# Attention stage of a one-core encoder layer: two heads in one PSUM bank, three masks moved to the selection stage, two more dense blocks woven in, and a choice among 17 orders

## The chip, the core and the metric

The kernel runs on one NeuronCore of one Trainium2 chip. A core has a matrix engine (TensorE, in the profile PE, with its weight loads as PEld), three engines for elementwise work (VectorE or DVE, ScalarE or ACT, GpSimd or POOL), and a SyncE (SP) that here issues every DMA. Each engine runs its own instructions in the order in which they were written and waits on semaphores for the others. The metric is the device time of one execution in microseconds (us); lower is better.

## The reference, cut to what matters

One layer of a streaming encoder: a SwiGLU feed-forward, a mixer with two attention branches, a second feed-forward. All in float32, 1024 tokens, width 1024. The change lies in the mixer:

```python
def fox_attention(q, k, v, log_f):            # 8 heads of 64, causal, with a forget bias
    F = jnp.cumsum(log_f, axis=1)
    ...
        s = jnp.einsum('bqhd,bkhd->bhqk', qb, k) * scale
        s = s + Fq[..., None] - F[:, :, None, :]
        s = jnp.where(mask, s, -jnp.inf)
        p = jax.nn.softmax(s, axis=-1)
        return jnp.einsum('bhqk,bkhd->bqhd', p, v)

def dsa_attention(q, k, v, iq, ik, iw, top_k):  # 8 heads, one shared k and v; each query attends
    ...                                         # to the 256 keys with the best index score
        score = jnp.einsum('bqh,bqhk->bqk', iwb, jax.nn.relu(dots))
        score = jnp.where(admissible[None], score, -jnp.inf)
        _, sel = lax.top_k(score, top_k)
    ...

merged = sigmoid(ga) * (ya @ w_br_fox) + sigmoid(gb) * (yb @ w_br_dsa)
return merged @ w_out
```

## The kernel before

**Two layers of program.** The functions of the kernel are generators that say what is computed, step by step. `weave` (line 2036) advances several of them side by side, in given proportions. While the plan is on, no instruction is emitted: `Plan.take` (215) records each as a `Task` with the tiles that it reads and writes and a rank, which is its number plus `nc.behind` (a lag that `behind`, 2072, sets for work of less urgency). At the end of a stage `Plan.flush` (519) orders all its tasks: `place` (318) simulates the engines with the durations of `takes` (450) or `length` (298), takes at each step the task that can start first, and breaks ties by rank. A task that needs a new tile may be placed only if its rank is at most `window` (600 here) above the lowest unplaced rank. `flush` makes two orders (with `takes` and no hold, with `length` and a hold of 0.05), passes each through `replay` (474), and emits the one whose TensorE ends first. All calls of one kind go through line 557, so the profile shows this line everywhere and rows are told apart by tile.

**Precision.** Each float32 operand is split into a rounded part hi (written by ScalarE) and a rest lo (VectorE, or GpSimd for some weights). A product is three matmuls: hi by hi, hi by lo, lo by hi (`mm3`, 589).

**The stages around the change.** Before the attention stage lies the *selection stage* (2433 to 2447): TensorE multiplies dense projections, while `topk` (977) finds the 256th best index score of each query. Query blocks 2 to 4 are searched bit by bit on VectorE (`rounds`), blocks 5 to 7 in two halves of 16 bits on ScalarE (`both`); the thresholds go into tile `thr`. Blocks 0 and 1 need no search, since they have at most 256 keys.

The *attention stage* (2453 to 2486) weaves three generators over 300 steps:
- attention: FoX's four pairs of heads, then DSA's four. For each pair and each two query blocks (j from 0 to 3) `att_scores` (1289) makes scores in PSUM tiles `p`, adds the forget bias or the mask with a minimum on VectorE (tile `pr`, `mn`), takes exp on ScalarE and normalizes on GpSimd. `att_values` (1337), for one head at a time, transposes `pr` through PSUM tiles `pt`, splits them into `pth` and `ptl` (`pzh` and `pzl` on the diagonal), and multiplies with the values into a PSUM tile `py` of which it uses 256 of 512 columns. The result leaves through tile `yt` (64x256) to `d_y` in HBM.
- `masks` (1076), in 40 parts of the 300 and 600 ranks behind: from the thresholds the masks of blocks 2 to 7, on VectorE, with tiles `tke`, `tky`, `tkg`, `tkn`. DSA needs them.
- dense work, 200 ranks behind, in 144 parts: `gates` (1214), 16 blocks of 24 matmuls of 512 columns for the second half of the tokens, then `Branches.first` (1943). The latter loads FoX's results from `d_y`, splits them into 16 tiles `h`, which are those that held the gates' operands, and multiplies the first two of eight output blocks of the FoX branch, gated with `d_gate`. Its raw data (weights `wbr`, results, gates) pass through two buffers `wr`; a weight's split goes over ScalarE (`wh`) and GpSimd (`wl`).

`pt`, `py` and the dense products share four PSUM banks (tag `pj`); `p` has the other four.

The *next stage* begins with `Branches.rest` (1969): blocks 2 to 7 of the FoX branch, the DSA results, the eight blocks of the DSA branch, then `w_out`. Its tensors use the memory that the attention stage leaves.

Of the kernel before, what the change touches and what calls it, by code (L numbers as in the profile page):

```python
# [22 lines left out]
D = 1024  # L23
# [171 lines left out]
class Plan:  # L195
# [19 lines left out]
    def take(self, engine, op, a, kw):  # L215
        if not self.on:
            return getattr(getattr(self.tc.nc, engine), op)(*map(real, a), **{n: real(v) for n, v in kw.items()})
        t = Task(len(self.tasks), engine, op, a, kw)
        t.rank, t.group = t.i + self.behind, max(0, self.group) if engine == "tensor" else 0
        self.tasks.append(t)  # L220
        writes = [v for v in (a[0], kw.get("accum_out")) if isinstance(v, View)]
        reads = [v for v in list(a[1:]) + [w for n, w in kw.items() if n != "accum_out"] if isinstance(v, View)]
        before = set()
        for views, write in ((reads, False), (writes, True)):
            for v in views:
                r = v.region()
# [24 lines left out]
        shape = list(out.shape)  # L251
        t.n = int(np.prod(shape[1:]))
        if op == "tensor_reduce":
            t.n = int(np.prod(a[1].shape[1:]))
        t.bytes = 4 * int(np.prod(shape))
        t.port = engine in ("vector", "gpsimd") and "accum_out" not in kw and not any(
            v.tile.pool.space == PSUM for v in reads + writes)
        if engine == "tensor":
            m = a[2] if op == "matmul" else a[1]
            t.exact = m.tile.dt in (F32R, BF16) or any(o[0] == "bitcast" and F32R in o[1] for o in m.ops)  # L260
            t.paired = op == "matmul" and a[1].region()[:1] == ((64, 128),)
            t.half = op == "matmul" and a[1].region()[:1] in (((64, 128),), ((0, 64),))
# [253 lines left out]
            free[e] = s + d  # L516
        return free

    def flush(self, keep=()):

        for x in keep:
            x.tile.uses += 1
# [16 lines left out]
            self.free, self.port, self.wire, self.kept = dict(st[3]), dict(st[4]), st[5], dict(st[6])  # L539

        at, best = state(), None
        for c in range(2):
            back(at)
            self.exact = not c
            order = self.place(0.05 * c)
            if order is None:
                continue
            free = self.replay(order, at[3], at[5])
            cost = free["tensor"]
            if best is None or cost < best[0]:  # L550
                best = (cost, order, state(), free)
# [188 lines left out]
def part8(w, c):  # L740

    return tuple(t[:, c * 128:c * 128 + 128] for t in w)
# [234 lines left out]
def topk(k, tmp):  # L977
# [90 lines left out]
    for i, _ in enumerate(rounds()):  # L1068
        if i % 2 == 0:
            next(b, None)  # L1070
        yield
    for _ in b:
        yield


def masks(k, tmp):


    nc = k.nc
    for qb in range(2, 8):  # L1080
        w = (qb + 1) * 128
        t, s = k.thr[:, qb - 2:qb - 1], k.s[qb]
        e, y = (tmp.tile([128, T], BF16, tag="tk" + x, name="tk" + x, bufs=1)[:, :w] for x in "ey")
        g = tmp.tile([128, T], F32, tag="tkg", name="tkg", bufs=1)[:, :w]
        need = tmp.tile([128, 2], F32, tag="tkn", name="tkn", bufs=2)
        nc.vector.tensor_scalar(e, s, t, None, op0=ALU.is_gt, op1=ALU.add, accum_out=need[:, 0:1])
        nc.vector.tensor_scalar(need[:, 1:2], need[:, 0:1], -1.0, float(TOPK), op0=ALU.mult, op1=ALU.add)
# [201 lines left out]
def att_scores(k, p, two, j, ps2):  # L1289
# [39 lines left out]
    for h in range(2):  # L1329
# [1 line left out]
            w, c = (2 * j + i + 1) * 128, 4 + 2 * i + h  # L1331
            nc.gpsimd.tensor_scalar(t[:, :w], t[:, :w], mn[:, c:c + 1], 1.0, op0=ALU.mult, op1=ALU.mult)
        yield
    two.pr = pr


def att_values(k, p, hd, j, pr, ps_t, ps_y):
    nc = k.nc
    py = ps_y()

    def pv(g, hi, lo):
        for i in range(2):
            kb = 2 * g + (1 - i if g == j else i)
            c = slice(i * 256, i * 256 + 256)
            end = g == j and i == 1
            if not end:
                nc.tensor.matmul(py[:, :256], hd.v(kb, 128), hi[:, c], start=g == 0 and i == 0, stop=False)
            nc.tensor.matmul(py[0:64, :256], hd.v(kb, 64), lo[:, c], start=False, stop=False)
            if end:
                nc.tensor.matmul(py[:, :256], hd.v(kb, 128), hi[:, c], start=False, stop=True)  # L1350

    last = None
    for g in range(j + 1):

        pt = ps_t(F32)
        if g == j:
            hi, lo = k.pz[k.pz_i % len(k.pz)]
# [11 lines left out]
        if last:  # L1369
            pv(*last)  # L1370
        yield
        last = (g, hi, lo)
    pv(*last)
    t = p.tile([64, 256], F32, tag="yt", name="yt", bufs=2)
    nc.scalar.activation(t, py[64:128, :256], AF.Copy)
    nc.vector.tensor_add(t, py[0:64, :256], t)
    nc.sync.dma_start(hd.y[:, j * 256:j * 256 + 256], t)
    yield


# [14 lines left out]
def pair_heads(k, p, kind, pr, ps_t, out):  # L1395
# [14 lines left out]
    else:  # L1410
# [2 lines left out]
        k.q2 = yield from two_heads(k, k.ap0, "qs", 4, lambda i: t[:, i, :], 2, None, ps_t)  # L1413
        two.kk = k.dks
        two.addend = lambda h, qb: k.mask[qb]
    two.q, two.heads = k.q2, []
    for h in range(2):
        hd = Head()
        hd.y = out[pr][h * 64:h * 64 + 64, :]
        if kind == "fox":  # L1420
            hd.v = lambda b, n, v=v[h]: v[:, b, 0:n]
        else:
            hd.v = lambda b, n: k.dvs[:, b, 0:n]
        two.heads.append(hd)
# [4 lines left out]
def attention(k, p, kind, npairs, out, ps2, ps_t, ps_y):  # L1429
# [3 lines left out]
    for pr in range(npairs):  # L1433
        two = k.ready
        prep = pair_heads(k, p, kind, pr + 1, ps_t, out) if pr + 1 < npairs else iter(())
        for j in range(4):
            yield from att_scores(k, p, two, j, ps2)
            for u in pend:
                yield from att_values(k, p, *u, ps_t, ps_y)
            pend = [(two.heads[h], j, two.pr[h]) for h in range(2)]  # L1440
            if j > 1:
                for _ in range(4):
                    next(prep, None)
# [109 lines left out]

PAIRS = NF // 2
NG = 6


class Operands:
# [369 lines left out]
class Branches:  # L1928
# [14 lines left out]
    def first(self, ws, ring, ptile):  # L1943

        k, nc = self.k, self.k.nc
        self.w, self.t = [next(ws) for _ in range(2)], []
        yield
        for pr in range(4):
            t = ring.raw()
            nc.sync.dma_start(t, k.d_y[0][pr])  # L1950
            for hf in range(2):
# [1 line left out]
                split(k, a, b, t[:, hf * H:hf * H + H])  # L1953
                self.y[hf].append((a, b))
                yield
        for i in range(2):
            g = ring.raw()
            nc.sync.dma_start(g, k.d_gate[i])
            for hf in range(2):
                ps = ptile()  # L1960
                self.product(ps, lambda c: part8(self.w[i], c), 0, hf)
                self.gated(g[:, hf * H:hf * H + H], ps)
                yield
            self.t.append(g)

    def kept(self):
        return [t for y in self.y for p in y for t in p] + [t for w in self.w for t in w] + self.t
# [1 line left out]
    def rest(self, pt1):  # L1969
# [14 lines left out]
            w = k.wq.split(k.wq.raw(self.wbr[d], br, home))  # L1984
            return lambda c: tuple(x[:, c % 4 * 128:c % 4 * 128 + 128] for x in w)

        for d in range(2, 8):
            w = half(d, 0, "c")
            for hf in range(2):
                t[d, hf] = gated(0, d, hf, w)  # L1990
            if d == 2:
# [107 lines left out]
def layer(tc, xT, c, pos, ada_w, ada_b, ng, inv, w13a, w2a, w_a, w_f, w_q, w_g, fb, fg, dg, wbr, wout, w13b, w2b, out):  # L2099
    with ExitStack() as es:  # L2100
# [51 lines left out]
        k.d_qkv = [dram([128, 8, 384], f"d_qkv{i}") for i in range(4)]  # L2152
        k.d_dq = [dram([128, 8, 128], f"d_dq{i}") for i in range(4)]
        k.d_gate = dram([16, 128, T], "d_gate")
        k.d_y = [[dram([128, T], f"d_y{b}{i}") for i in range(4)] for b in range(2)]

        s1 = ExitStack()
# [275 lines left out]
        with ExitStack() as ph:  # L2433
# [14 lines left out]
        ws.parts, ws.n = [(d_wg[b], D, r2) for b in range(2, 16)] + [(wbr[b], D, r2) for b in range(2)], 1  # L2448
        fox.close()
        s1.close()  # L2450

# [4 lines left out]
        with ExitStack() as ph:  # L2456
            ap = pool(ph, "att", True)
            ap.lay(("zero", 128, F32, 1), ("pzh", H, F32R, 2), ("pzl", H, F32R, 2), ("pth", H, F32R, 3), ("ptl", H, F32R, 3),
                   ("yt", 256, F32, 2), ("f", T, F32, 2), ("vst", T, F32R, 2), ("qs", T, F32R, 2), ("mn", 8, F32, 6))
            mp = pool(ph, "masks", True)  # L2460
            ap.p.tile([128, 16], F32, name="pad4")
            pt = lambda dt: pq.tile([128, H], dt, tag="pj", name="pt", bufs=4)
# [19 lines left out]
                yield from attention(k, ap, "dsa", 4, k.d_y[1], p2, pt, py)  # L2482

            br = Branches(k, wbr)
            weave((chain(attention(k, ap, "fox", 4, k.d_y[0], p2, pt, py), dsa()), 300), (behind(nc, masks(k, mp), 600), 40), (behind(nc, chain(gates(k, ws, 1, GateTiles(ap, py)), br.first(ws, r2, py)), 200), 144))
            nc.flush(br.kept())
        ps.close()
        s3.close()

# [136 lines left out]
```

## Time and profile before

| | us |
|---|---|
| median of 3 runs | 2172.49 |
| lowest, highest | 2171.11, 2172.92 |
| the profiled execution | 2171.82 |
| its span, from the first to the last instruction | 2170.1 |

The profile covers one execution. A row of the grouped views names engine, operation, output<-inputs and shape; times on the axis count from the span's start. TensorE is counted as busy from a matmul's start to its modelled end, so neighbouring matmuls overlap and a busy share near 100% doesn't say that matmuls follow each other as closely as they can. The number of matmuls in a stretch says that. The selection stage ends at about 1006 us, the attention stage with `Branches.first` at about 1362 us. The last gate of the attention stage, the first load into `wr` after it and what follows there are read from the views by tile; the rows stand where they are used.

### The profile page before, as it was taken

To read this page: it belongs to the slowest core of one execution; us is meant where nothing else is said; L and a number is where in the kernel's file an instruction comes from. 1 tells how busy PE (TensorE), PEld (TensorE's weight loads), DVE (VectorE), ACT (ScalarE), POOL (GpSimd) and SP (SyncE) were. 2 spreads that over 40 slices of the span, in tenths; PEclk is the share of its full clock that TensorE was granted. 3 is DMA by queue.
4 is the path that set the end of the run, shared out by engine and by line. 5 is a ranking of instruction groups with operands and counts; after the bars stand their busy time and mean duration, and the time that the engine had idled before them with its cause. 6 is when DMAs were issued, how large, how long until landed. Compare 5 with 4: busy or idle time off the path is not lost. (4 is left out here: it accounts for less than half of the span.)

```text
span 2170.1 us, 31523 instructions
## 1 busy us (share of the span) xinstructions
PE 2130.4 (98%) x10700; PEld 1777.6 (82%) x10700; DVE 1616.0 (74%) x3095; ACT 1130.3 (52%) x2103; POOL 221.3 (10%) x229
## 2 busy tenths in 40 slices
PE   7999999999999999999999999999999999999999
PEld 5887888887888989997778877888788888888887
DVE  7977887789876499964996777598866756558665
ACT  5744444445455466785766777244543333334443
POOL 0000212210010110111342333000000000000000
PEclk9999999999999999999999999999999999999999
DMA  9245887799521444356343312696123532367521
GB/s 337 99 136 180 274 286 260 243 366 337 158 81 60 146 153 141 103 188 221 108 151 106 125 48 82 233 358 189 58 81 126 174 122 83 107 232 273 175 73 39
DMA packets 208622, 364.15 MB, mean 168 GB/s; under 512 B 29622, under 2 KB 57270, under 8 KB 208460
## 3 DMA queue, kind: packets, MB, share of 16 engines
q1 hardware_dynamic: 208460, 362.13, 49.2%
q8 instruction: 84, 1.38, 0.3%
q14 instruction: 78, 0.64, 0.1%
HBM read 265.85 MB, written 96.20 MB: 167 GB/s over the span
## 5 line engine op out<-in xcount | busy, mean ns | idle before, releaser
L557 PE MATMUL bs<-h,wh 128*128 128x512 f32 x1728 | 533.6, 391 | 2.2 <-ACT bs L557 1.3
L557 ACT ACTIVATE wh<-wr 128x512 fp32r<-128x512 f32 (+1 forms) x330 | 207.5, 639 | 347.6 <-PE bs L557 158.4
L557 PEld LDWEIGHTS bs<-h,wh 128*128 128x128 f32 x1728 | 323.6, 188 | 73.1 <-ACT bs L557 4.3
L557 PE MATMUL b<-h,wh 128*128 128x512 f32 x1088 | 339.0, 392 | 3.2 <-ACT z L557 1.6
L557 PE MATMUL bs<-h,wl 128*128 128x512 f32 x864 | 335.5, 390 | 0.6 <-DVE wl L557 0.6
L557 DVE TENSOR_TENSOR wl<-wr,wh 128x512 fp32r<-128x512 f32 x308 | 210.6, 701 | 121.4 <-ACT wh L557 116.7
L557 PEld LDWEIGHTS b<-h,wh 128*128 128x128 f32 x1088 | 204.4, 188 | 48.0 <-ACT z L557 2.4
L557 PE MATMUL b<-h,wl 128*128 128x512 f32 x544 | 212.5, 391 | 0.9 <-DVE wl L557 0.9
L557 PEld LDWEIGHTS bs<-h,wl 128*128 128x128 f32 x864 | 162.3, 188 | 35.0 <-DVE wl L557 1.1
L557 PE MATMUL pj<-wh,h 128*128 128x384 f32 (+1 forms) x768 | 178.4, 319 | 0.0
L557 ACT ACTIVATE wh<-a 128x512 fp32r<-128x512 f32 x132 | 83.2, 631 | 168.2 <-PE b L557 93.3
L557 DVE TENSOR_TENSOR wl<-a,wh 128x512 fp32r<-128x512 f32 x132 | 92.5, 701 | 84.8 <-ACT wh L557 81.3
L557 PE MATMUL b<-wh 128*128 128x512 f32 x352 | 137.4, 390 | 0.7 <-ACT mrow L557 0.7
L557 PE MATMUL b<-wh,wl 128*128 128x512 f32 x352 | 137.2, 390 | 0.0
L557 PE MATMUL b<-wl,wh 128*128 128x512 f32 x352 | 137.2, 390 | 0.0
L557 PEld LDWEIGHTS pj<-wh,h 128*128 128x128 f32 x768 | 132.5, 189 | 0.3
L557 PE MATMUL pj<-wl,h 128*128 128x384 f32 (+1 forms) x384 | 122.0, 318 | 0.0
L557 PEld LDWEIGHTS b<-h,wl 128*128 128x128 f32 x544 | 102.5, 188 | 22.7 <-DVE wl L557 1.3
L557 DVE TENSOR_TENSOR z<-bs,z 128x512 f32<-128x512 f32 x116 | 79.3, 686 | 49.8 <-PE bs L557 29.1
L557 POOL TENSOR_SCALAR pr<-pr,mn 128x128 f32<-128x128 f32 (+7 forms) x128 | 98.4, 788 | 170.5 <-DVE mn L557 138.6
L557 DVE TENSOR_TENSOR wl<-g,wh 128x512 fp32r<-128x512 f32 x154 | 107.0, 695 | 4.0 <-ACT wh L557 4.0
L557 ACT ACTIVATE pr<-pr,mn 128x256 f32<-128x256 f32 (+7 forms) x128 | 98.6, 772 | 16.7 <-DVE mn L557 16.0
(321 smaller groups left out, 4290.6 us busy)
## 6 DMA issues: line engine op xcount, KB each, us to landing
d_g<-z SPq DMA_DIRECT2D x154, 256.0 KB, 2.6
g<-d_g SPq DMA_DIRECT2D x154, 256.0 KB, 4.0
mraw<-in_ada_w SPq DMA_DIRECT2D x144, 256.0 KB, 5.2
wr<-in_w13a SPq DMA_DIRECT2D x112, 256.0 KB, 5.0
wr<-in_w13b SPq DMA_DIRECT2D x88, 256.0 KB, 4.6
a<-in_w2a SPq DMA_DIRECT2D x44, 256.0 KB, 5.3
a<-in_w2b SPq DMA_DIRECT2D x44, 256.0 KB, 5.3
gw<-in_w_g SPq DMA_DIRECT2D x32, 256.0 KB, 5.3
```

Source lines behind the costliest of these rows:

```text
L557: getattr(getattr(self.tc.nc, e), t.op)(*map(real, t.a), **{n: real(v) for n, v in t.kw.items()})
```

## The change

- `att_values` takes both heads of a pair. It goes through (g, h) for the key blocks g and heads h, both heads accumulate in one `py` (columns 0 to 255 and 256 to 511), and one `yt` of 64x512 carries both to `d_y`, with one DMA. Only head 0's first matmul clears the bank.
- The masks of blocks 2 to 4 are made in `topk`'s last steps, in the selection stage, with tiles of that stage. The attention stage makes blocks 5 to 7 only.
- `Branches.first` multiplies blocks 2 and 3 of the FoX branch too (`EARLY`), ahead of blocks 0 and 1, and stores their gated result in a new HBM buffer `d_t`. `rest` loads it from there and starts its own products at block 4. The dense generator gets 155 parts in place of 144, and `first` no longer takes its two weights at its start.
- The lag of a task is kept apart from its number. For the attention stage `flush` tries 15 more orders, in which all lags are multiplied by 0 to 3.

```diff
@@ take
-        t.rank, t.group = t.i + self.behind, max(0, self.group) if engine == "tensor" else 0
+        t.lag, t.group = self.behind, max(0, self.group) if engine == "tensor" else 0
@@ flush
-    def flush(self, keep=()):
+    def flush(self, keep=(), pulls=()):
...
-        for c in range(2):
+        for exact, f in ((True, 1.0), (False, 1.0)) + tuple((True, x) for x in pulls):
             back(at)
-            self.exact = not c
-            order = self.place(0.05 * c)
+            self.exact = exact
+            for t in tasks:
+                t.rank = t.i + t.lag * f
+            order = self.place(0.0 if exact else 0.05)
@@ topk, masks
+    m = masks(k, tmp, range(2, 5), (("tkj", 640), ("tke", T)), 640)
     for _ in b:
+        next(m, None)
         yield
-
-
-def masks(k, tmp):
+    for _ in m:
+        yield
+
+
+def masks(k, tmp, qbs, tags, n=T):
...
-    for qb in range(2, 8):
+    for qb in qbs:
...
@@ att_values
-def att_values(k, p, hd, j, pr, ps_t, ps_y):
+def att_values(k, p, two, j, ps_t, ps_y):
     nc = k.nc
     py = ps_y()
 
-    def pv(g, hi, lo):
+    def pv(h, g, hi, lo):
+        hd, o = two.heads[h], slice(256 * h, 256 * h + 256)
...
-                nc.tensor.matmul(py[:, :256], hd.v(kb, 128), hi[:, c], start=g == 0 and i == 0, stop=False)
-            nc.tensor.matmul(py[0:64, :256], hd.v(kb, 64), lo[:, c], start=False, stop=False)
+                nc.tensor.matmul(py[:, o], hd.v(kb, 128), hi[:, c], start=h == 0 and g == 0 and i == 0, stop=False, **kw)
+            nc.tensor.matmul(py[0:64, o], hd.v(kb, 64), lo[:, c], start=False, stop=False, **kw)
...
-    for g in range(j + 1):
-
+    for g, h in ((g, h) for g in range(j + 1) for h in range(2)):
+        pr = two.done[j][h]
...
-    t = p.tile([64, 256], F32, tag="yt", name="yt", bufs=2)
-    nc.scalar.activation(t, py[64:128, :256], AF.Copy)
-    nc.vector.tensor_add(t, py[0:64, :256], t)
-    nc.sync.dma_start(hd.y[:, j * 256:j * 256 + 256], t)
+    t = p.tile([64, H], F32, tag="yt", name="yt", bufs=2)
+    nc.scalar.activation(t, py[64:128, :], AF.Copy)
+    nc.vector.tensor_add(t, py[0:64, :], t)
+    nc.sync.dma_start(two.y[:, j * 256:j * 256 + 256].rearrange("(h p) q -> p h q", h=2),
+                      t.rearrange("p (h q) -> p h q", h=2))
@@ Branches.first
-        self.w, self.t = [next(ws) for _ in range(2)], []
-        yield
+        self.t = []
...
-        for i in range(2):
+        for i in list(range(2, 2 + EARLY)) + [0, 1]:
+            if i == 0:
+                self.w = [next(ws) for _ in range(2)]
+            w = next(ws) if i > 1 else self.w[i]
             g = ring.raw()
             nc.sync.dma_start(g, k.d_gate[i])
             for hf in range(2):
                 ps = ptile()
-                self.product(ps, lambda c: part8(self.w[i], c), 0, hf)
+                self.product(ps, lambda c: part8(w, c), 0, hf)
                 self.gated(g[:, hf * H:hf * H + H], ps)
                 yield
-            self.t.append(g)
+            if i > 1:
+                later(k, 1, lambda i=i, g=g: nc.sync.dma_start(k.d_t[i], g))
+                tick(k)
+            else:
+                self.t.append(g)
@@ Branches.rest
-        for d in range(2, 8):
+        for d in range(2, 2 + EARLY):
+            for hf in range(2):
+                t[d, hf] = t512(k, name="gr")
+                nc.sync.dma_start(t[d, hf], k.d_t[d][:, hf * H:hf * H + H])
+        for d in range(2 + EARLY, 8):
...
@@ layer, attention stage
-            weave((chain(attention(k, ap, "fox", 4, k.d_y[0], p2, pt, py), dsa()), 300), (behind(nc, masks(k, mp), 600), 40), (behind(nc, chain(gates(k, ws, 1, GateTiles(ap, py)), br.first(ws, r2, py)), 200), 144))
-            nc.flush(br.kept())
+            weave((chain(attention(k, ap, "fox", 4, k.d_y[0], p2, pt, py), dsa()), 300), (behind(nc, masks(k, mp, range(5, 8), (("tke", T), ("tky", T))), 600), 40), (behind(nc, chain(gates(k, ws, 1, GateTiles(ap, py)), br.first(ws, r2, py)), 200), 155))
+            nc.flush(br.kept(), [0.0, 0.25, 0.5, 0.625, 0.75, 0.875, 1.125, 1.25, 1.375, 1.5, 1.75, 2.0, 2.25, 2.5, 3.0])
```

More of the change, by code (lines that the diff above doesn't have):

```diff
@@ L1071, in topk @@
         yield
+    m = masks(k, tmp, range(2, 5), (("tkj", 640), ("tke", T)), 640)
     for _ in b:
+        next(m, None)
         yield
-def masks(k, tmp):
+    for _ in m:
+        yield
+def masks(k, tmp, qbs, tags, n=T):
     nc = k.nc
-    for qb in range(2, 8):
+    for qb in qbs:
         w = (qb + 1) * 128
         t, s = k.thr[:, qb - 2:qb - 1], k.s[qb]
-        e, y = (tmp.tile([128, T], BF16, tag="tk" + x, name="tk" + x, bufs=1)[:, :w] for x in "ey")
-        g = tmp.tile([128, T], F32, tag="tkg", name="tkg", bufs=1)[:, :w]
+        e, y = (tmp.tile([128, m], BF16, tag=x, name="tk" + x, bufs=1)[:, :w] for x, m in tags)
+        g = tmp.tile([128, n], F32, tag="tkg", name="tkg", bufs=1)[:, :w]
         need = tmp.tile([128, 2], F32, tag="tkn", name="tkn", bufs=2)
@@ L1333, in att_scores @@
         yield
-    two.pr = pr
-def att_values(k, p, hd, j, pr, ps_t, ps_y):
+    two.done[j] = pr
+def att_values(k, p, two, j, ps_t, ps_y):
     nc = k.nc
     py = ps_y()
-    def pv(g, hi, lo):
+    def pv(h, g, hi, lo):
+        hd, o = two.heads[h], slice(256 * h, 256 * h + 256)
+        kw = dict(skip_group_check=True) if h else {}
         for i in range(2):
@@ L1346, in pv @@
             if not end:
-                nc.tensor.matmul(py[:, :256], hd.v(kb, 128), hi[:, c], start=g == 0 and i == 0, stop=False)
-            nc.tensor.matmul(py[0:64, :256], hd.v(kb, 64), lo[:, c], start=False, stop=False)
+                nc.tensor.matmul(py[:, o], hd.v(kb, 128), hi[:, c], start=h == 0 and g == 0 and i == 0, stop=False, **kw)
+            nc.tensor.matmul(py[0:64, o], hd.v(kb, 64), lo[:, c], start=False, stop=False, **kw)
             if end:
-                nc.tensor.matmul(py[:, :256], hd.v(kb, 128), hi[:, c], start=False, stop=True)
+                nc.tensor.matmul(py[:, o], hd.v(kb, 128), hi[:, c], start=False, stop=True, **kw)
     last = None
-    for g in range(j + 1):
+    for g, h in ((g, h) for g in range(j + 1) for h in range(2)):
+        pr = two.done[j][h]
         pt = ps_t(F32)
@@ L1371, in att_values @@
         yield
-        last = (g, hi, lo)
+        last = (h, g, hi, lo)
     pv(*last)
-    t = p.tile([64, 256], F32, tag="yt", name="yt", bufs=2)
-    nc.scalar.activation(t, py[64:128, :256], AF.Copy)
-    nc.vector.tensor_add(t, py[0:64, :256], t)
-    nc.sync.dma_start(hd.y[:, j * 256:j * 256 + 256], t)
+    t = p.tile([64, H], F32, tag="yt", name="yt", bufs=2)
[3 more added lines that the diff above has]
+                      t.rearrange("p (h q) -> p h q", h=2))
     yield
@@ L1415, in pair_heads @@
         two.addend = lambda h, qb: k.mask[qb]
-    two.q, two.heads = k.q2, []
+    two.q, two.heads, two.y, two.done = k.q2, [], out[pr], {}
     for h in range(2):
         hd = Head()
-        hd.y = out[pr][h * 64:h * 64 + 64, :]
         if kind == "fox":
@@ L1439, in attention @@
                 yield from att_values(k, p, *u, ps_t, ps_y)
-            pend = [(two.heads[h], j, two.pr[h]) for h in range(2)]
+            pend = [(two, j)]
             if j > 1:
@@ L1555 @@
 NG = 6
+EARLY = 2
 class Operands:
@@ L1990, in rest @@
                 t[d, hf] = gated(0, d, hf, w)
-            if d == 2:
+            if d == 2 + EARLY:
                 for hf in range(2):
@@ L2154, in layer @@
         k.d_gate = dram([16, 128, T], "d_gate")
+        k.d_t = {i: dram([128, T], f"d_t{i}") for i in range(2, 2 + EARLY)}
         k.d_y = [[dram([128, T], f"d_y{b}{i}") for i in range(4)] for b in range(2)]
@@ L2447, in layer @@
             nc.flush(k.hh[1] + k.hl[1] + k.q2 + k.k2 + [t for w in ws.q for t in w])
-        ws.parts, ws.n = [(d_wg[b], D, r2) for b in range(2, 16)] + [(wbr[b], D, r2) for b in range(2)], 1
+        ws.parts, ws.n = [(d_wg[b], D, r2) for b in range(2, 16)] + [(wbr[b][:, 0:H], H, r2) for b in range(2, 2 + EARLY)] + [(wbr[b], D, r2) for b in range(2)], 1
         fox.close()
@@ L2458, in layer @@
             ap.lay(("zero", 128, F32, 1), ("pzh", H, F32R, 2), ("pzl", H, F32R, 2), ("pth", H, F32R, 3), ("ptl", H, F32R, 3),
-                   ("yt", 256, F32, 2), ("f", T, F32, 2), ("vst", T, F32R, 2), ("qs", T, F32R, 2), ("mn", 8, F32, 6))
+                   ("yt", H, F32, 2), ("f", T, F32, 2), ("vst", T, F32R, 2), ("qs", T, F32R, 2), ("mn", 8, F32, 6))
             mp = pool(ph, "masks", True)
```

## The prediction, made before the change was run

> **What bounds the kernel now.** I read the page first: busy time by engine, then the chain that ended last.
>
> ```profile
> span 2170.1 us, 31523 instructions
> PE 2130.4 (98%) x10700; PEld 1777.6 (82%) x10700; DVE 1616.0 (74%) x3095; ACT 1130.3 (52%) x2103; POOL 221.3 (10%) x229
> ...
> PE 43%; DVE 2%; ACT 2%; issue 1%; DMA 0%; DVEq 0%; ACTq 0%
> ```
>
> TensorE is the bound. None of the change's edits removes a matmul, so time can come only out of stretches in which PE does less than it could. "98% busy" hides these, since a matmul counts as busy while it drains. I therefore counted matmuls per stretch, for the selection stage's end (956 to 1006), the attention stage (1006 to 1362), its sequel, and one dense stretch.
>
> ```profile
> 956.00:1006.00 50.00, 50.00 (x320) 45.48 (x319) 30.73 (x96) 37.11 (x69) 2.57 (x2) 1.00 0.45 145
> 1006.00:1019.50 13.50, 12.70 (x65) 9.65 (x65) 0.63 (x4) 2.23 (x4) 2.21 (x2) 1.00 1.01 332
> 1019.50:1040.00 20.50, 18.06 (x133) 13.71 (x131) 17.91 (x50) 15.88 (x40) 8.81 (x14) 1.00 0.65 234
> 1040.00:1140.00 100.00, 97.96 (x708) 79.10 (x707) 91.34 (x192) 69.90 (x155) 37.45 (x41) 1.00 0.44 136
> 1140.00:1289.00 149.00, 148.31 (x1052) 121.35 (x1051) 101.10 (x236) 103.02 (x233) 46.39 (x63) 1.00 0.30 98
> 1289.00:1340.00 51.00, 44.60 (x315) 35.29 (x314) 43.07 (x98) 42.52 (x94) 17.35 (x21) 0.97 0.25 82
> 1340.00:1362.00 22.00, 21.73 (x123) 18.39 (x124) 10.60 (x19) 9.38 (x18) 4.71 (x4) 0.92 0.29 87
> 1362.00:1380.00 18.00, 17.39 (x77) 14.06 (x76) 12.52 (x20) 8.23 (x14) 0.00 (x0) 1.00 1.04 383
> 1736.00:1790.00 54.00, 54.00 (x239) 44.14 (x238) 28.00 (x46) 19.16 (x34) 0.00 (x0) 1.00 0.38 123
> ```
>
> The columns are the stretch, its length, then busy time and instructions of PE, PEld, DVE, ACT and POOL, the granted clock, DMA share and rate. The same stretches, for the matmuls alone that read tile h (the dense gate and branch products, each 512 columns wide), on PE:
>
> ```profile
> 1006.00:1019.50 13.50, 11.62 (x49) 1.00 1.01 332
> 1019.50:1040.00 20.50, 2.58 (x12) 1.00 0.65 234
> 1040.00:1140.00 100.00, 37.62 (x130) 1.00 0.44 136
> 1140.00:1289.00 149.00, 64.94 (x206) 1.00 0.30 98
> 1289.00:1340.00 51.00, 0.00 (x0) 0.97 0.25 82
> 1340.00:1362.00 22.00, 13.07 (x47) 0.92 0.29 87
> ```
>
> A dense matmul costs 54.00 / 239 = 0.226 us. In 1140 to 1289, where PE is nearly full, 206 of them take 46.5 us, which leaves 102.5 us for 846 attention matmuls: 0.121 us each. With these two prices I value the other stretches. 1289 to 1340: 315 x 0.121 = 38.2 of 51 us, so **12.8 us are empty**. 1340 to 1362: 47 x 0.226 + 76 x 0.121 = 19.8 of 22, 2.2 empty. 1019.5 to 1040: 12 x 0.226 + 121 x 0.121 = 17.4 of 20.5, 3.1 empty. 1040 to 1140: 0.6. 1006 to 1019.5: 0.5. Together 19.2 us. The sequel from 1362 on is full (77 x 0.226 = 17.4 of 18), and so is 956 to 1006.
>
> The large hole is the one without a single dense matmul. There, attention alone sets the pace, with DVE at 43.07 and ACT at 42.52 of 51 us. Two of PE's waits there (1290 to 1345; in total, times, longest), both for an attention tile's split:
>
> ```profile
> PE py L557 <- ACT pth L557: 1.5, 3, 0.9
> PE py L557 <- DVE pzl L557: 1.1, 1, 1.1
> ```
>
> **The change part by part.**
>
> *Two more dense blocks inside.* 2 blocks x 2 halves x 12 = 48 matmuls, 10.8 us of PE, leave the full stretch after 1362 and become filler for the attention stage. Their worth is the hole they fill: 12.8 / 0.226 = 57 matmuls would close it. But filler must also be there in time. By tile, the gates' last step, and then all that passes through the wr buffers from 1290 on:
>
> ```profile
> L557 ACT ACTIVATE gt<-py x16: 574/594/603, 1016.1 to 1288.7; 128x512 f32<-128x512 f32 x16
> ```
>
> ```profile
> L557 DVE TENSOR_TENSOR h<-wr,h x8: 671/677/693, 1320.1 to 1342.4; 128x512 fp32r<-128x512 f32 x8
> L557 SPq DMA_DIRECT2D wr<-d_y x4: 320/326/406, 1311.7 to 1329.3; - x4
> ...
> L557 ACT ACTIVATE wh<-wr x2: 632/840/1048, 1315.8 to 1361.4; 128x1024 fp32r<-128x1024 f32 x1, 128x512 fp32r<-128x512 f32 x1
> ...
> L557 POOL TENSOR_TENSOR wl<-wr,wh x1: 2377/2377/2377, 1316.9 to 1316.9; 128x1024 fp32r<-128x1024 f32 x1
> ...
> DMA to landing us min/median/max: 3.1/3.2/4.1
> ```
>
> Each row of these two tables gives shortest, median and longest duration in ns and the first and last start; the last line is of the loads into wr.
>
> The last gate block ends at 1288.7. Only then can FoX's results be split into the 16 h tiles that the gates' operands occupied. That starts with a load at 1311.7 and ends at 1342.4, four loads of 512 KB through two wr buffers, so the first branch product comes at 1340. The change puts the eight splits and the first products at steps 145 to 155 of 155 of the weave, where all were appended behind it: about 10/155 of the 356 us stage, 23 us earlier by an even pace (an estimate). The first load would then come at about 1289 and the first product at about 1318. The gates also move up in program order, by 11/155, but holes have pulled them ahead of it already (206 in 149 us is 1.38 per us, an even 384 over 356 us is 1.08); I take their end as nearly unmoved, at 1285. The hole shrinks from 51 to some 33 us: 18 x 12.8/51 = **4.5 us** gained. Bounds: 0 (both ends move alike) and 12.8 (the planner finds filler for all of it). Behind the hole 96 branch matmuls (21.7 us) instead of 48 lie beside the attention's end: of the 2.2 us there I take **1.0**.
>
> What the two blocks add there: 4 gatings on DVE at about the 0.68 us of its 512-wide operations, two ACT splits, two POOL splits of half the 2.38 us above, and on SP two weight loads, two gate loads and two stores of 512 KB, later four reloads of 256 KB in place of the gate loads that leave. Those reloads come first in the next stage's program and can hold SP there for a store that hasn't landed; behind them on SP stand the weights of block 4 and DSA's results, for which PE would wait. DMA is saturated then (share 1.04). A store of this size is not in the trace; the nearest row is that of the 512 KB loads, 3.2 and at most 4.1 us. PE's cover behind it falls from six branch blocks to four, 4 x 5.4 = 21.7 us, still more than one load. Between 0 and 4.1 us I take a **loss of 1.0**.
>
> *Masks of blocks 2 to 4 in the selection stage.*
>
> ```profile
> L557 DVE TENSOR_TENSOR thr<-tkkey,tkm x1: 155/155/155, 955.5 to 955.5; 128x3 uint32<-128x3 uint32 x1
> ...
> 1019.00:1145.00 126.00, 30.71 (x36) 1.00 0.47 152
> ...
> L557 DVE TENSOR_SCALAR tky<-s,thr 128x384 bf16<-128x384 f32 (+5 forms) x6 | 3.5, 589 | 0.0
> ...
> 1019.55 0.29 DVE L557 CUSTOM_DVE_ANT_0 pr<-p,f 128x128 f32<-128x128 f32 x1 [12.88 <-DMA f<-d_f]
> ```
>
> The six masks cost 30.71 (DVE's operations on tile tke) + 3.5 = 34.2 us, all in 1019 to 1145; by columns blocks 2 to 4 have 1536 of 4224, 12.4 us. Their threshold is ready at 955.5. From there to 1006 DVE is idle for 50 - 30.7 = 19.3 us, and then for 12.9 us more until the f load lands, while PE is full in the first stretch and nearly so in the second. So the moved work costs nothing; without that cover it would delay the first scores by up to 12.4 us. Attention's start gets DVE relief: 17.9 + 91.3 = 109.3 busy of 120.5 us falls to 96.9. Of the 3.7 us empty there (1019.5 to 1140) part is the pipeline's filling, which stays; I take half, **1.9** (bounds 0 and 3.7).
>
> *Two heads in one PSUM bank.* The matmuls stay. 64 evictions of 64x256 become 32 of 64x512:
>
> ```profile
> L557 ACT ACTIVATE yt<-py x64: 365/380/384, 1029.1 to 1355.3; 64x256 f32<-64x256 f32 x64
> L557 DVE TENSOR_TENSOR yt<-py,yt x64: 386/410/418, 1029.7 to 1355.7; 64x256 f32<-64x256 f32 x64
> ```
>
> With the 512-wide rows above as price (gt on ACT, h on DVE) a pair saves 2 x 0.380 - 0.594 = 0.17 us on ACT and 2 x 0.410 - 0.677 = 0.14 on DVE. That counts only in the hole, where these engines set the pace and some five pairs fall: **0.7**. Elsewhere PE covers it. SP issues 32 stores fewer.
>
> [...] The present price of a late eviction:
>
> ```profile
> PE pt L557 <- DVE yt L557: 1.4, 2, 0.8
> ```
>
> [...]
>
> *Order from 17 plans.* The first two are today's; 15 more scale how far gates, branches and masks lag. A plan is taken only if its own replay ends earlier. I take **1.5** (bounds 0 and what the other terms leave of 19.2); a replay that misjudges the chip could cost as much.
>
> Sum: 4.5 + 1.0 - 1.0 + 1.9 + 0.7 + 1.5 = 8.6 us. The profiled execution took 2171.8 us (span 2170.1 and 1.7 around it), 0.7 below the median 2172.5: 2171.8 - 8.6 = **2163**.
>
> On the clock: it falls to 0.97 and 0.92 in two stretches where PE's longest wait is the 1.1 us quoted, worth 0.03 x 51 + 0.08 x 22 = 3.3 us, already within the empty time. [...]
>
> **The rivals.**
> - *The hole closes wholly*: the chosen lag spreads the gates so that the h tiles change hands without a gap. 12.8 + 2.2 + 1.9 + 0.7 - 1.0 = 16.6, 2155. For it: 48 + 48 matmuls are more than the 57 missing. Against: the split chain takes 30 us, on engines at 84%.
> - *The change does not do what it says; the hole only moves*: gates and splits both come earlier, and the added filler is spent in front of or behind the hole. Then masks and evictions remain, 1.9 + 0.7 - 1.0: 2170, within 2168 to 2176.
> - *Slower: the two wr buffers become the bound.* Twelve loads and two stores pass through them instead of eight, and the weights of blocks 0 and 1 now come last. If those are late when attention ends, PE waits for store 3.2, load 4.1, ACT 1.1 and POOL 2.4: 10.8 us, and half as much for the second block, 16 in all against 8.6 won: 2179. It decides once the fourth block's operands are ready later than the last attention matmul (1355 today); for it speaks that four y loads took 18 us to issue.
>
> **How the numbers follow.** The forecast (2158 to 2168) has 0.52, the closed hole 0.20, the moved hole 0.18, slower 0.10. About 0.2% (4.3 us) can be told from no change: faster 0.72, same 0.18, slower 0.10. The range 2153 to 2172 leaves out the slower case, the upper part of "same", and little below.
>
> **What would show it.** Dense matmuls between 1289 and 1340, no 50 us stretch without them, fewer dips of the clock; DVE under 85% in 1020 to 1140 and mask rows before 1006; 32 yt rows of 64x512 near 0.6 and 0.7 us; the stage's work larger by 48 matmuls with under 12 us empty. It is wrong if the wl rows or SP's waits set PE's start after attention ends, or the empty time stays near 19 us.

## The result and the profile after

The changed kernel takes **2158.1 us** (median of 4 runs, 2156.0 to 2159.6), the kernel before 2172.7 in the same series (4 runs, 2171.1 to 2174.4). The ratio is 0.9932, 95% interval 0.9915 to 0.9949: 14.6 us faster. The profiled execution took 2159.6 us, 12.2 less than that of before. The forecast was 2163 within 2153 to 2172.

First the page of the changed kernel, busy time by engine and the chain that ended last:

```profile
span 2157.9 us, 31319 instructions
PE 2123.0 (98%) x10700; PEld 1772.5 (82%) x10700; DVE 1611.6 (75%) x3061; ACT 1125.8 (52%) x2071; POOL 226.4 (10%) x231
...
PE 88%; DVE 5%; DMA 3%; ACT 2%; issue 1%; SPq 0%; POOL 0%; DVEq 0%; ACTq 0%; POOLq 0%
```

PE still bounds, with as many matmuls (10700) and the same busy share, and 88% of the chain is PE's. As before, the time has to be looked for by counting matmuls per stretch. The same windows as in the prediction (length, then busy time and instructions of PE, PEld, DVE, ACT, POOL, clock, DMA share and rate), and the matmuls alone that read tile h:

```profile
1006.00:1019.50 13.50, 12.78 (x66) 9.90 (x66) 2.92 (x16) 1.85 (x4) 0.06 (x1) 1.00 0.98 330
1019.50:1040.00 20.50, 19.04 (x137) 14.76 (x135) 15.12 (x41) 15.45 (x39) 9.25 (x14) 1.00 0.71 252
1040.00:1140.00 100.00, 99.47 (x737) 81.75 (x736) 86.15 (x178) 72.06 (x155) 41.78 (x46) 1.00 0.43 134
1140.00:1289.00 149.00, 148.79 (x1052) 122.34 (x1052) 102.70 (x227) 103.72 (x224) 45.72 (x62) 1.00 0.36 115
1289.00:1340.00 51.00, 48.46 (x344) 39.31 (x344) 39.88 (x86) 38.78 (x79) 20.94 (x23) 1.00 0.31 102
1340.00:1360.00 20.00, 19.52 (x114) 16.16 (x113) 8.45 (x13) 7.61 (x13) 2.20 (x3) 1.00 0.39 111
```

```profile
1006.00:1019.50 13.50, 11.57 (x50) 1.00 0.98 330
1019.50:1040.00 20.50, 4.20 (x19) 1.00 0.71 252
1040.00:1140.00 100.00, 38.82 (x124) 1.00 0.43 134
1140.00:1289.00 149.00, 68.40 (x214) 1.00 0.36 115
1289.00:1340.00 51.00, 14.77 (x48) 1.00 0.31 102
1340.00:1360.00 20.00, 11.24 (x48) 1.00 0.39 111
```

With the prediction's prices (0.226 us for a dense matmul, 0.121 for one of attention) the empty time is:

| stretch | before | after |
|---|---|---|
| 1006 to 1140 | 0.5 + 3.1 + 0.6 = 4.2 | 0.3 + 1.9 - 2.2 = 0.0 |
| 1140 to 1289 | 0 (prices are from here) | -0.8 |
| 1289 to 1340, the hole | 12.8 | 51 - 48 x 0.226 - 296 x 0.121 = 4.3 |
| from 1340 to the stage's end | 2.2 | 1.2 |
| sum | 19.2 | 4.7 |

A negative value means that the mix of attention matmuls was a little cheaper than the mean price. So 14.5 us were won inside the stage: 8.5 in the hole, 4.2 at the start, 1.0 at the end, 0.8 between. The next stage gave some back: PE waits there for 1.3 + 0.2 us, before for 0.6.

```profile
PE b L559 <- ACT yh L559: 1.3, 1, 1.3
...
PE b L559 <- ACT wh L559: 0.2, 1, 0.2
```

14.5 - 0.9 = 13.6, between the 12.2 of the two profiled executions and the 14.6 of the medians. By tile (shortest, median, longest duration in ns, first and last start), first the last dense and the last attention product of the stage, then what the prediction named as signs:

```profile
L559 PE MATMUL py<-h,wl x160: 387/395/496, 1012.9 to 1359.5; 128*128 128x512 f32 x160
```

```profile
L559 PE MATMUL py<-pzh,vst x128: 277/283/389, 1029.0 to 1349.2; 128*128 128x256 f32 x128
```

```profile
L559 ACT ACTIVATE gt<-py x16: 574/595/605, 1018.2 to 1286.9; 128x512 f32<-128x512 f32 x16
```

```profile
L559 ACT ACTIVATE h<-wr x8: 617/619/626, 1273.7 to 1293.3; 128x512 fp32r<-128x512 f32 x8
...
L559 SPq DMA_DIRECT2D wr<-d_y x4: 319/324/586, 1226.5 to 1285.5; - x4
L559 SPq DMA_DIRECT2D d_t<-wr x2: 319/322/326, 1302.8 to 1328.1; - x2
```

```profile
L559 ACT ACTIVATE yt<-py x32: 593/594/597, 1031.4 to 1349.5; 64x512 f32<-64x512 f32 x32
L559 DVE TENSOR_TENSOR yt<-py,yt x32: 654/682/684, 1032.5 to 1350.1; 64x512 f32<-64x512 f32 x32
```

```profile
L559 DVE TENSOR_TENSOR_SCAN tkg<-tktkj x3: 953/1225/1492, 973.3 to 983.2; 128x384 f32<-128x384 bf16 x1, 128x512 f32<-128x512 bf16 x1, 128x640 f32<-128x640 bf16 x1
```

The gates end where they did (1286.9, before 1288.7). But FoX's results are loaded from 1226.5 and split on ScalarE from 1273.7, while the last gate still runs, and not from 1311.7 and 1319.4. The scans of the masks of blocks 2 to 4 lie at 973 to 985, and all steps of these masks between 962 and 987, before the selection stage ends. PE's wait for a late eviction fell from 1.4 us in two waits to 0.4 in one:

```profile
PE py L559 <- DVE yt L559: 0.4, 1, 0.4
```

### The profile page after: what moved, and what is told of

The parts are those of the page before. It is cut to its first block, busy times and chain, and to the rows that moved or that the text cites. A ratio compares the mean times of both kernels' runs of the same rounds, so it can differ in the third digit from the quotient of the medians.

```text
span 2157.9 us, 31319 instructions
## 1 busy us (share of the span) xinstructions
PE 2123.0 (98%) x10700; PEld 1772.5 (82%) x10700; DVE 1611.6 (75%) x3061; ACT 1125.8 (52%) x2071; POOL 226.4 (10%) x231
## 4 chain that ended last, share of the span: by engine, by line
PE 88%; DVE 5%; DMA 3%; ACT 2%; issue 1%; SPq 0%; POOL 0%; DVEq 0%; ACTq 0%; POOLq 0%
PE bs L559 34%; PE b L559 27%; PE pj L559 12%; PE py L559 8%; PE p L559 3%; PE pt L559 3%; DVE xc L559 1%; DMA a<-in_w2a 1%; DVE wl L559 1%; DVE xb L559 1%; DMA g<-d_g 1%; DMA gw<-in_w_f 0%; DVE pr L559 0%; SPq L559 0%; DVE z L559 0%
## 5 line engine op out<-in xcount | busy, mean ns | idle before, releaser
L559 PE MATMUL b<-h,wh 128*128 128x512 f32 x1072 | 334.2, 391 | 3.4 <-ACT z L559 1.6
L559 PE MATMUL py<-h,wh 128*128 128x512 f32 x320 | 113.2, 406 | 1.0 <-DVE wr L559 0.7
```

Of the source, the lines that this page charges most:

```text
L559: getattr(getattr(self.tc.nc, e), t.op)(*map(real, t.a), **{n: real(v) for n, v in t.kw.items()})
```

## The experiments

Twelve kernels, each with the changed kernel or the kernel before as its base and one thing altered. This table comes first since the readings below go back to it. *End* is the start of the stage's last matmul in the trace; kernels that lack the two more blocks have 10.8 us (48 x 0.226) added, so that all have done the same work. *Wait* is PE's wait for the first operands of the next stage.

| run | median us | ratio to before, 95% | end | wait | span |
|---|---|---|---|---|---|
| before | 2172.7 | 1 | 1373.0 | 0.6 | 2170.1 |
| changed | 2158.1 | 0.9932 (0.9915 to 0.9949) | 1359.5 | 1.5 | 2157.9 |
| no_plans | 2162.4 | 0.9957 (0.9944 to 0.9969) | 1363.2 | 1.1 | 2160.7 |
| branch_at_end | 2167.4 | 0.9984 (0.9975 to 0.9993) | 1362.5 | 5.2 | 2166.4 |
| no_more_blocks | 2166.1 | 0.9974 (0.9966 to 0.9983) | 1362.1 | 7.3 | 2167.3 |
| before_155 | 2174.5 | 1.0011 (1.0003 to 1.0020) | 1368.5 | 4.2 | 2170.6 |
| masks_back | 2163.1 | 0.9962 (0.9948 to 0.9976) | 1361.0 | 2.2 | 2159.8 |
| no_bank | 2167.8 | 0.9979 (0.9970 to 0.9988) | 1366.9 | 2.4 | 2165.7 |
| reloads_later | 2158.1 | 0.9935 (0.9922 to 0.9947) | 1359.7 | 0.4 | 2156.7 |
| spread | 2155.7 | 0.9927 (0.9914 to 0.9939) | 1357.0 | 0.4 | 2154.0 |
| two_evictions | 2176.1 | 1.0022 (1.0013 to 1.0031) | 1375.3 | 2.2 | 2174.0 |
| bank_only | 2165.4 | 0.9973 (0.9964 to 0.9982) | 1369.2 | none | 2165.4 |
| filler_only | 2169.9 | 0.9992 (0.9984 to 1.0001) | 1371.1 | 0.7 | 2168.2 |
| plans_only | 2167.6 | 0.9984 (0.9975 to 0.9993) | 1365.1 | 0.8 | 2162.8 |

Span less end less wait is 796.2 to 796.9 in eleven of the fourteen and 797.9 to 798.7 in the three whose wait is over 4 us. So each time is the sum of two things: **when the stage ends and how long PE then waits**. The kernel before had medians of 2171.1 to 2172.7 in the four series. Runs of one kernel differ by 1 to 8 us and a trace shows one of them (for plans_only the shortest, for no_more_blocks the longest), so the medians carry the sizes and the traces the places.

Two limits hold for all that follows. The changed kernel ran in the first series only, so a loss against it compares medians of different series. By the ratios no_plans, branch_at_end, no_more_blocks, masks_back and no_bank lose 5.4, 11.3, 9.1, 6.5 and 10.2 us in place of the 4.3, 9.3, 8.0, 5.0 and 9.7 given below, and the interval of the changed kernel's own ratio reaches 3.7 us to each side. And where the 17 orders are kept, the planner chooses again in each kernel, so the edit changes the order too. Its replay takes all lags times 1.25 in the changed kernel, branch_at_end, no_more_blocks and reloads_later, but times 0.75 in masks_back and plans_only, 0.875 in two_evictions, 2 in spread and 2.25 in no_bank.

### First series: place, filler, choice

The theory was PLACE: what counts is that the branch work moved from behind all attention into the weave. Rivals were the 48 products as such (SUPPLY) and the 15 more orders (CHOICE).

**no_plans**
```diff
-            nc.flush(br.kept(), [0.0, 0.25, ..., 3.0])
+            nc.flush(br.kept())
```


> The changed kernel with the old choice between two orders, all else kept. The changed kernel took 2158.1 us, the one before 2172.7. Theory PLACE (most of the gain comes from where FoX's results and the first branch products stand in the program: inside the weave, at about three quarters of the attention stage's tasks, in place of behind all of them): within 3 us of the changed kernel, 2157 to 2161; the prediction's own term for the choice was 1.5 us, so 2159.6. Rival CHOICE (the 15 more orders carry it): 2165 to 2171, and the 50 us stretch without dense matmuls ahead of the branch products is back.

It lost 4.3 us and lies between the two expected ranges: the choice (here lags times 1.25 in place of 1) is worth more than the forecast's 1.5 and far less than all. No hole came back; 48 dense matmuls still lie between 1289 and 1340.

**branch_at_end**
```diff
-... br.first(ws, r2, py)), 200), 155))
+... br.first(ws, r2, py)), 200), 144))
```


> The changed kernel with the dense generator's parts set back from 155 to 144, so that the sixteen gate blocks alone fill the weave and the y loads, their splits and all eight half products of the FoX branch are appended behind all attention, as before; masks, shared bank, the two more blocks and the 17 orders stay. Theory PLACE: half or more of the gain is lost, 2165 to 2170, with a stretch of 30 us or more without dense matmuls after the last gate. Rival SUPPLY (the 48 more dense matmuls fill the hole wherever they stand): at most 2161. Rival CHOICE: the scaled lags make up for the place, at most 2161.

The time is in PLACE's range, but not for its reason. The stage ends only 3.0 us later and 33 dense matmuls lie in the hole, where the theory had a long stretch without any; most of the rest is a new wait. PE's waits (in all, times, longest) and SP's issues, in order of time:

```profile
PE b L559 <- ACT wh L559: 5.2, 1, 5.2
```

```profile
1354.53 0.32 SPq L559 DMA_DIRECT2D d_t<-wr  x1
1358.07 0.80 SPq L559 DMA_DIRECT2D wr<-d_gate  x2
1358.91 0.90 SPq L559 DMA_DIRECT2D gr<-d_t  x2
1359.86 0.43 SPq L559 DMA_DIRECT2D wr<-in_wbr  x1
```

The store of block 3's result goes out at 1354.5, its reload is issued at 1358.9, and only behind it the weight of the first block that the next stage multiplies. Split, it is there for PE at 1368.1, 5.2 us after the end of the stage's last product (start 1362.5, 0.4 long).

**no_more_blocks**
```diff
-EARLY = 2
+EARLY = 0
```


> The changed kernel with no blocks beyond 0 and 1 inside (the constant for the early blocks at 0, so 48 dense matmuls go back to the next stage and the stores and reloads of their results are gone); 155 parts, masks, shared bank and the 17 orders stay. Theory PLACE: within 3 us of the changed kernel, 2156 to 2161, since splits and first products still stand inside the weave. Rival SUPPLY: 48 x 0.226 = 10.8 us go back behind a stage that ends no earlier, 2166 to 2170.

8.0 us lost, SUPPLY's size, and again not by its path. For the same work the stage ends 2.6 us later, not 10.8, and PE waits 7.3. The last dense product starts at 1328.6 here, before attention ends, so that nothing lies over the next stage's first loads:

```profile
L559 PE MATMUL py<-h,wl x144: 387/393/506, 1015.1 to 1328.6; 128*128 128x512 f32 x144
```

```profile
PE b L559 <- ACT wh L559: 7.3, 1, 7.3
```

**before_155**
```diff
-... br.first(ws, r2, py)), 200), 144))
+... br.first(ws, r2, py)), 200), 155))
```


> The kernel before with one number changed: 155 parts for the dense generator in place of 144, so that the y loads, the splits and the first two half products of the FoX branch stand inside the weave. Two orders, masks, banks and blocks as before. Theory PLACE: half or more of the gain, 2162 to 2166, and dense matmuls between 1295 and 1335 us of the span. Rival SUPPLY or CHOICE: at most 3 us, 2170 to 2173.

No theory's result: by the ratio 2.4 us *slower* (0.7 to 4.3). PLACE falls. The loads into wr start at 1259.3, while the gates still run:

```profile
L557 ACT ACTIVATE gt<-py x16: 577/596/603, 1017.5 to 1271.8; 128x512 f32<-128x512 f32 x16
```

```profile
L557 SPq DMA_DIRECT2D wr<-d_y x4: 319/326/326, 1259.3 to 1277.1; - x4
```

But the first branch products go out before 1289, and the hole is as empty of dense matmuls as it was (matmuls on tile h):

```profile
1289.00:1340.00 51.00, 0.00 (x0) 1.00 0.10 28
1340.00:1362.00 22.00, 7.41 (x24) 1.00 0.18 51
```

The stage ends 4.5 us earlier all the same, and the wait of 4.2 and what follows it take that back. Some 3.3 of the 4.5 us are the two dips of the clock in the kernel before (0.97 and 0.92 in the prediction's rows), which this run does not have (1.00 above).

The new theory, HANDOVER: the next stage's first weight is requested when SP is through with the attention stage's last store and whatever stands in front of it (in before_155 SP's last stores end at 1357.6 and the weight's load follows at 1357.7). Dense products behind the last attention product hide what follows. In the changed kernel those are the 10.3 us between 1349.2 and 1359.5.

### Second series: masks, bank, handover, a better spread

**masks_back**
```diff
-    m = masks(k, tmp, range(2, 5), ...)
-        next(m, None)
...
-... masks(k, mp, range(5, 8), ...)
+... masks(k, mp, range(2, 8), ...)
```


> The changed kernel with the masks of blocks 2 to 4 made in the attention stage again, as before; place of the branch work, two more blocks, shared bank and the 17 orders stay. The changed kernel took 2158.1 us. The prediction's term for the masks is 1.9: 2160, within 2158 to 2163. Rival COVERED (VectorE's masks lie beside a full TensorE anyway, the choice of order finds them a place): at most 2159. Rival LOAD (the 12.4 us of VectorE work count in full, since attention waits for VectorE): 2166 or more.

5.0 us by the medians, of which the traces account for 1.9 (spans 2159.8 and 2157.9): the trace of masks_back is of its shortest run, that of the changed kernel of its longest. The median lies at the upper end of the expected range. VectorE is busy for 90.91 of the 100 us (changed kernel: 86.15), and PE gets 722 matmuls done there against 737.

```profile
1040.00:1140.00 100.00, 99.07 (x722) 81.03 (x722) 90.91 (x186) 71.39 (x154) 41.98 (x43) 1.00 0.43 136
```

**no_bank**: `att_values` of before, called for one head at a time.
```diff
-    for g, h in ((g, h) for g in range(j + 1) for h in range(2)):
+    for g in range(j + 1):
...
-            pend = [(two, j)]
+            pend = [(two.heads[h], j, two.done[j][h]) for h in range(2)]
```


> The changed kernel with one head per PSUM bank again: 64 evictions of 64x256 and 64 stores in place of 32 and 32; all else of the change stays. The prediction's term for the eviction is 0.7: 2159, within 2157 to 2161. [...]

9.7 us lost, fourteen times the term, though the other order may have a part in it. The expectation misses. The stage ends 7.4 us later:

```profile
1040.00:1140.00 100.00, 98.10 (x710) 79.55 (x709) 81.30 (x175) 71.26 (x156) 34.61 (x41) 1.00 0.45 148
```

27 matmuls fewer than in the changed kernel, though 133 of them are dense, in place of 124. By the prediction's prices that is 2.3 us: the loss begins where PE is busy for 98% of the time and seems covered.

**reloads_later**
```diff
-        for d in range(2, 2 + EARLY):
-            ... nc.sync.dma_start(t[d, hf], k.d_t[d][...])
         for d in range(2 + EARLY, 8):
...
+        for d in range(2, 2 + EARLY):
+            ... nc.sync.dma_start(t[d, hf], k.d_t[d][...])
         for d in range(8):
```


> The changed kernel with the four reloads of the early blocks' results issued behind the loads for blocks 4 to 7 and not ahead of them; nothing else. Theory HANDOVER (the next stage's first weight is loaded only when SP has issued the attention stage's last store and what stands between, and TensorE waits for it unless dense products still lie behind the last attention product): the four reloads hold SP 2.2 us ahead of that load, and PE's waits of 0.2 and 1.3 us there go: 1 to 1.8 us off, 2156 to 2157. Rival: the wait for the split of the DSA results has another cause (ScalarE, or the rate of the DMA), 2158.

The wait falls from 1.5 to 0.4, as HANDOVER says. The median, 2158.1, is the rival's number and doesn't show it; 1.1 us is within what runs of one kernel differ by.

**spread**
```diff
-            weave((chain(attention(...), dsa()), 300), ... 155))
+            weave((chain(attention(...), dsa()), 320), ... 156))
```


> The reloads issued later as in the run before, and the attention given 320 steps and the dense work 156 parts in place of 300 and 155, so that the last gates and the branch products lie some 6% later in the program and reach further into the attention stage's end, while about 10 us of dense products still lie behind its last result. Theory PLACE AND SUPPLY (the empty time left between 1289 and 1360 is where dense products run out): 2 to 4 us off the run before, 2152 to 2155, with no wait over 0.5 us for the next stage's first weight. Rival: what is left empty is the pipeline's own latency, 2156 to 2158.

2155.7 (2154.5 to 2157.7), 2.3 below the run before it in the same series: within the expected 2 to 4, though above the 2152 to 2155 that had counted on a gain from the reloads. It is the fastest of all, though the intervals of its ratio and the changed kernel's overlap. The hole is closed, 74 x 0.226 + 283 x 0.121 = 51.0 of 51 us (all matmuls, then those on tile h):

```profile
1289.00:1340.00 51.00, 50.78 (x357) 42.12 (x356) 40.41 (x85) 40.05 (x83) 24.68 (x24) 1.00 0.36 122
```

```profile
1289.00:1340.00 51.00, 22.82 (x74) 1.00 0.36 122
```

### Third series: each part alone

**two_evictions**
```diff
+    for h in range(2):
+        t, o = p.tile([64, 256], ...), slice(256 * h, 256 * h + 256)
+        nc.scalar.activation(t, py[64:128, o], AF.Copy)
+        nc.vector.tensor_add(t, py[0:64, o], t)
+        nc.sync.dma_start(two.y[h * 64:h * 64 + 64, ...], t)
```


> The changed kernel with both heads still in one PSUM bank and their matmuls in the same order, but evicted as two tiles of 64x256 each, with two stores, as before: 64 rows on ScalarE, 64 on VectorE. Without any sharing the kernel took 2167.8 us, with it 2158.1. Theory EVICTION (the 32 x 0.17 us on ScalarE and 32 x 0.14 on VectorE are what sharing saves): near the kernel without sharing, 2164 to 2168. Rival ORDER (what counts is that the two heads alternate and hold one bank in place of two, so that a split has longer time and banks come free for dense products): within 3 us of the changed kernel, 2157 to 2161.

Slower than without sharing, by 8.3. It brought a wait of its own, so it does not tell EVICTION from ORDER:

```profile
PE py L559 <- ACT yt L559: 6.6, 18, 0.5
PE py L559 <- DVE yt L559: 2.7, 5, 1.1
```

Head 0's half is copied as soon as it is done, and head 1's products into the same bank wait for the copy: 9.3 us in 23 waits. The planner did not foresee this, since it compares the columns that two tasks touch and not the bank. What the chip would do without these waits was not tried.

**bank_only**: the shared bank alone, in the kernel before.

> The kernel before with the shared bank alone: heads alternating, one bank, 32 evictions. The kernel before took 2171.1 to 2171.5 us in the last two series. The prediction's term was 0.7: 2170.5, within 2169 to 2172. Rival ALONE (the 9.7 us that the changed kernel loses without it are its own worth): 2160 to 2164.

6.0 us by the medians, 5.9 by the ratio (3.9 to 7.8): between the expectations, nearer to ALONE. Its stretches, all matmuls, then those on tile h:

```profile
1040.00:1140.00 100.00, 96.92 (x709) 80.06 (x706) 90.46 (x187) 69.22 (x147) 40.77 (x43) 0.98 0.42 133
1140.00:1289.00 149.00, 148.30 (x1054) 120.97 (x1052) 103.66 (x229) 102.99 (x227) 45.38 (x64) 1.00 0.32 101
1289.00:1340.00 51.00, 45.39 (x334) 37.93 (x333) 42.05 (x88) 40.99 (x86) 23.05 (x25) 0.97 0.26 81
```

```profile
1040.00:1140.00 100.00, 37.50 (x121) 0.98 0.42 133
1140.00:1289.00 149.00, 62.90 (x197) 1.00 0.32 101
1289.00:1340.00 51.00, 5.87 (x19) 0.97 0.26 81
```

From 1040 to 1289 attention does 588 + 857 = 1445 matmuls (before 578 + 846 = 1424) and takes 318 dense ones as filler (before 336). The 18 that it didn't need lie in the hole: 19 there, before none. That is no matter of the clock: its 0.98 and 0.97 are worth 0.02 x 100 + 0.03 x 51 = 3.5 us, the two dips of before 3.3. Why attention gets ahead with less filler (less engine time, alternating heads, one change of hands per bank and pair) was not separated.

**filler_only**: 155 parts and the two more blocks alone.

> The kernel before with the place and the two more blocks alone: 155 parts and 48 more dense products in the attention stage; masks, banks and the choice between two orders as before. The prediction's terms for these were 4.5 + 1.0 - 1.0: 2167, within 2165 to 2169. Rival ALONE (what the changed kernel loses without the place, 9.3, or without the blocks, 8.0, is their own worth): 2160 to 2163. Rival TOGETHER (they count only beside the other parts): 2170 to 2173.

1.5 us by the medians, 1.7 by the ratio (-0.2 to 3.5): TOGETHER nearly, and not the forecast's 4.5. Between 1289 and 1340 lie eight dense matmuls:

```profile
1289.00:1340.00 51.00, 46.74 (x332) 36.67 (x331) 39.87 (x95) 38.30 (x87) 16.71 (x22) 0.97 0.17 54
```

```profile
1289.00:1340.00 51.00, 1.71 (x8) 0.97 0.17 54
```

**plans_only**: the 15 more orders alone.

> The kernel before with the choice among 17 orders alone. The prediction's term was 1.5: 2169.6, within 2168 to 2171. Rival ALONE (the 4.3 us that the changed kernel loses without the choice are its own worth): 2166 to 2168. Rival HANDOVER (an order that ends the stage earlier, with few dense products behind the last attention result, makes PE wait for the next stage's first weight): 2171 or more, with a wait of over 2 us for it.

3.8 us by the medians, 3.5 by the ratio (1.5 to 5.4), near what leaving it out costs (4.3). ALONE holds for this part; the handover wait is 0.8.

## Why the prediction was right and wrong

**Right in sign and near in size; its sum of terms was not.** 8.6 us were forecast, 14.6 came, between the forecast's own case and *the hole closes wholly*. That the sum came this near is partly luck: alone, place and blocks gave 3.0 us less than their terms, bank and orders 7.6 more.

- **The bound and the place.** That time could come only out of stretches with too few matmuls, and that the one from 1289 to 1340 is the largest, held: 8.5 of the 14.5 us come from there. All listed signs appeared: 48 dense matmuls in the hole, no dip of the clock, VectorE at (15.12 + 86.15) / 120.5 = 84%, 32 evictions near 0.6 and 0.7 us.
- **The term 4.5 for the place and the filler failed** as a step. "Only then can FoX's results be split" was wrong: the changed kernel splits while the last gate runs, and before_155 loads at 1259.3. What held the loads of before until 1311.7 was the program, as before_155 shows by its loads. The weave's 300 steps are not the whole stage: by the program's numbering of the tasks the last gate is 2688 of 3532 and FoX's loads come from 3455 on, behind all attention, out of the planner's window of 600; in the changed kernel they start at 2613 of 3477. So the place moved much further than the "10/155 of the stage". And earlier was no gain in itself: alone, it only moved the hole (the rival of that name; before_155), and with the two blocks it measured 1.5, not 4.5 + 1.0 - 1.0. The planner spends filler on any gap that comes first.
- **The term 0.7 for the evictions failed most**: 6.0 alone, 9.7 within the change. The failing sentence is "That counts only in the hole ... Elsewhere PE covers it". A PE at 98% busy is not covered: by bank_only's counts, the faster attention comes through there, the fewer dense matmuls it uses up that are missing later. PE's wait for evictions did not grow in the changed kernel: 1.4 us before, 0.4 after.
- **The masks**: 1.9 forecast. The start's empty time fell from 4.2 to 0.0, and to 0.9 + 2.0 - 0.8 = 2.1 in masks_back, so about 2 of that are theirs; by the medians they are worth 5.0. The traces, the shortest run of one against the longest of the other, don't show where the rest lies, and the order is another one. That they cost nothing in the selection stage held: PE's 320 matmuls between 956 and 1006 are unchanged.
- **The choice of the order**: 1.5 forecast, 3.5 and 4.3 measured; mis-sized, with the right sign.
- **The clock**: the prediction counted two dips, 3.3 us, within the empty time. They were won back, so that much of the 14.5 us is clock. What sets a dip off was not separated: before_155, with as few dense matmuls in the hole, has none in the stage, bank_only has two.
- **The next stage**: -1.0 forecast, 0.9 more wait seen, and in reloads_later's trace it goes when the reloads no longer stand ahead of block 4's weight on SP. What the prediction missed is how thin the cover is. "Four branch blocks" hide later loads, not the first one; for that one only the dense products behind attention's end count, and where they were fewer or SP was held, 4.2 to 7.3 us appeared.
- **The rival with two wr buffers** did not come: the last wr store starts at 1328.1, 21 us before attention ends. Its relative, a store that holds SP, showed in branch_at_end with 5.2 us.

The parts don't add up in a fixed way. Alone, bank, orders and filler give 6.0 + 3.8 + 1.5 (the masks were not tried alone); left out, the bank costs 9.7, place 9.3, blocks 8.0. Most of the last two is the handover wait, which the whole change happens to hide.

## To carry to other kernels

Where a planner fills gaps with independent work, count that work as a stock: a part that makes the main chain steadier early leaves filler for the end, and more or earlier filler alone is spent on the first gaps. Split a stage's time into its end for equal work and the wait at the next stage's first load, and keep some independent work behind the last result as cover for that load. Leaving one part out measures also what that part hides, so try each part alone as well.

## What the runs showed of the hardware

In these runs TensorE's granted clock fell to about a half behind a wait of 7.3 us, and also where no wait was over 0.7. In no_more_blocks PE is nearly empty from 1351.5 to 1359.0 (0.25 us busy, three matmuls) and the granted clock is 0.52 in the next 3.4 us:

```profile
1351.50:1359.00 7.50, 0.25 (x3) 0.12 (x1) 0.77 (x2) 2.71 (x4) 0.00 (x0) 0.76 0.62 149
1359.00:1362.40 3.40, 3.40 (x9) 2.68 (x10) 1.90 (x3) 1.95 (x4) 0.00 (x0) 0.52 1.00 377
```

Half of 3.4 us is 1.7, about what the three runs with a wait over 4 us have too much in the table (797.9 to 798.7, the others 796.2 to 796.9). The other two show a low clock there as well: branch_at_end 0.50 in the 3.4 us from 1367.7, before_155 0.75 and 0.82 in the two stretches of 4 us from 1360. The kernel before has the same episode behind 5 us in which PE is busy for 3.51 and no wait is over 0.7 us:

```profile
1298.00:1303.00 5.00, 3.51 (x29) 2.33 (x26) 4.02 (x12) 4.98 (x12) 1.37 (x2) 1.00 0.05 13
1303.00:1306.50 3.50, 3.50 (x19) 3.50 (x19) 1.25 (x3) 1.20 (x4) 2.82 (x3) 0.54 0.02 5
```

The first pair of rows has a stretch ahead of the low clock that is nearly idle, the second one that is sparse and not idle. In the changed kernel's attention stage, with dense matmuls in all six stretches, the granted clock is 1.00 in each of them.
